# Ten feed-forward blocks by seven products in place of nine, with one of the weight sums added by a DMA

## The chip, the cores and the metric

The kernel runs on one core of a Trainium2 chip. A core has a matrix engine (TensorE, in the profile PE, its weight loads PEld), three engines for elementwise work (VectorE = DVE, ScalarE = ACT, GpSimd = POOL) and a sync engine (SyncE = SP) that here only issues DMAs. The metric is the time of one execution on the device in microseconds; three runs of the kernel before gave a median of 1944.8 us (1944.8 to 1944.86).

## What is computed

Two decoder layers over 256 tokens of width 2048, all in float32. Cut to what matters here:

```python
h  = rms_norm(x, norm1_g[l]);  z = h @ w_in[l]          # then SGU and attention
x  = x + mixed @ w_out[l]
h2 = rms_norm(x, norm2_g[l])
x  = x + (silu(h2 @ w_gate[l]) * (h2 @ w_up[l])) @ w_down[l]
```

`w_gate` and `w_up` are 2048 x 5632, `w_down` is 5632 x 2048. The change is in the last line only.

## The kernel before

**Precision.** A float32 product is made of three matmuls in a rounded float32 form: each operand is split in a high part and a low rest (`ah`, `al`; `wh`, `wl`), and `mm3` (lines 137 to 140) adds high*high, high*low and low*high in PSUM. So every tile of weights has to be split on its way to TensorE: `split2` (lines 93 to 104) has ScalarE make `wh` by a cast (L99) and VectorE make `wl` by a subtraction (L100). There are five buffers each for `wh` and `wl`. Weights arrive as raw tiles of 128 x 1024 (512 KB), seven buffers, loaded by SP (`raw_load`, L90).

**Blocks.** The 5632 columns of the feed-forward part are eleven blocks of 512. For a block, gate and up can be computed in two ways.
- *Standard* (`half`, `even`): 8 raw tiles of `w_gate` and 8 of `w_up`, each a unit of 12 matmuls. 192 matmuls, 16 splits.
- *Seven products* (`seven`, lines 608 to 680): the tokens (two groups of 128), the rows of the weights (even and odd groups of 256) and the two matrices (gate, up) make a 2 x 2 by 2 x 2 product of blocks, done with seven block products in place of eight. The price is sums of weight tiles. B11 and B12 are the even rows of gate and up (`b11`, `b12`), B21 and B22 the odd ones (`b21`, `b22`). There are four steps (`i`), each with five units of 6 matmuls: product 0 of `b11`, product 1 of `b11 + b12`, product 3 of `t2 = b11 + b12 + b22`, product 2 of `b12 + b22`, product 4 of `b22`. VectorE makes the three sums at L636, L637 and L642, in place in the raw tiles but for `t2`. After `t2` has been split for product 3, GpSimd issues a DMA that adds `b21` to it in place (L644, an accumulating DMA). After the four steps eight more units use `b21` (loaded again) and the four `t2`. In all 7 x 24 = 168 matmuls, 28 splits, 12 sums and 7 small operations on VectorE; standard has 2 of these.

Blocks 2 to 10 are made by seven products (`S_BLOCKS`), 0 and 1 the standard way.

**Order.** `s_stream` yields after each unit of the seven-product blocks. Between its units the loop at the end of the layer inserts units of the other stream (`std_stream`, ordered by `STD_ORDER`: gate and up of the standard blocks, and the products with `w_down`, "down", 12 matmuls for one split) as long as a tally of VectorE's work is ahead of TensorE's: `vec` adds 1.14 us for each sum or split, `pe` takes off 0.227 us x `LOAD` for each matmul. The resulting order is fixed when the program is built, and each engine takes its instructions in that order. A raw tile's buffer comes free when its last split is done, and SP, which issues the loads in order, waits for that.

Of the kernel before, what the change touches and what calls it, by code (L numbers as in the profile page):

```python
# [16 lines left out]
ALU = mybir.AluOpType  # L17
# [22 lines left out]
NI = 3584 // NB  # L40
NFF = DFF // NB
ND = D // NB
S_BLOCKS = (2, 3, 4, 5, 6, 7, 8, 9, 10)
STD_ORDER = (
    ("gu", 0), ("down", (0, 2)), ("down", (3, 4)), ("gu", 1), ("down", (1, 5)), ("down", (6, 7)), ("down", (8, 9)), ("down", (10,)),
)
ACTS = 6
HOLD = 2
VEC = 1.14
VEC_P = 0.6  # L50
MM = 0.227
LOAD = 0.95
RL = 512
WARM = 12

# [12 lines left out]
def trunk(ctx, tc, x, xt, w_in, w_out, w_gate, w_up, w_down, sgu_w, sgu_g, consts,  # L68
          rel_bias, onehot, radd, out):
    nc = tc.nc  # L70
# [15 lines left out]
    def raw_load(src, parts=1):  # L86
        raw = wp.tile([P, 2, NB], F32, tag="raw", name="raw", bufs=7)
        n = 2 // parts
        for i in range(parts):
            nc.sync.dma_start(raw[:, i * n : (i + 1) * n, :], src[:, i * n : (i + 1) * n, :])  # L90
        return raw

    def split2(raw):
        wh = wp.tile([P, 2, NB], F32R, tag="wh", name="wh", bufs=5)
        wl = wp.tile([P, 2, NB], F32R, tag="wl", name="wl", bufs=5)
        step = 2 if clock[0] > 1 else 1
        for j in range(0, 2, step):
            src = raw[:, j : j + step, :]
            nc.scalar.copy(wh[:, j : j + step, :], src)  # L99
            nc.vector.tensor_tensor(  # L100
                wl[:, j : j + step, :], src, f(wh[:, j : j + step, :]), ALU.subtract
            )
        vec(1)
        return wh, wl
# [3 lines left out]

    def vec(n, cost=VEC):
        debt[0] += n * cost  # L110

    def pe(n):
        debt[0] -= n * MM * LOAD

# [6 lines left out]
    def tick(w=1.0):  # L121
        clock[0] += w
        due = sorted((e for e in pending if e[0] <= clock[0]), key=lambda e: e[:2])
        pending[:] = [e for e in pending if e[0] > clock[0]]
        for e in due:
            e[2]()
# [10 lines left out]
    def mm3(acc, ah, al, wh, wl, first, last, **more):  # L137
        nc.tensor.matmul(acc, ah, wh, start=first, stop=False, **more)  # L138
        nc.tensor.matmul(acc, ah, wl, start=False, stop=False, **more)  # L139
        nc.tensor.matmul(acc, al, wh, start=False, stop=last, **more)  # L140
# [134 lines left out]
    for lay in range(L):  # L275
# [324 lines left out]
        def act_later(b, sg, held=held, admit=admit):  # L600
            def come(c):
                held.append((b, c, sg))
                admit()

            for c in range(2):
                later(2 + c, lambda c=c: come(c))

        def seven(b, lay=lay, pairs2=pairs2, ext2=ext2, act_later=act_later):
            bank = {}

            def s_unit(raw, m, i, op, first, last, **more):
                wh, wl = split2(raw)
                if m not in bank:
                    bank[m] = pa.tile([P, NB], F32, tag="acc", name=f"m{m}")
                for j in range(2):
                    ah, al = (op(2 * i + j, h) for h in range(2))
                    mm3(bank[m], ah, al, wh[:, j, :], wl[:, j, :], first and j == 0, last and j == 1, **more)
                pe(6)
                tick(0.5)

            def a_op(k, t):
                return lambda p, h: pairs2[p][:, h, k, t * P : (t + 1) * P]

            def e_op(n):
                return lambda p, h: ext2[p][:, h, n, :]

            kept = []
            for i in range(4):
                b11 = raw_load(w_gate[lay, b, i, 0])
                b12 = raw_load(w_up[lay, b, i, 0])  # L630
                b22 = raw_load(w_up[lay, b, i, 1])
                t2 = ap.tile([P, 2, NB], F32, tag="spt", name="t2", bufs=4)
                first, last = i == 0, i == 3
                s_unit(b11, 0, i, a_op(0, 0), first, last)
                yield
                nc.vector.tensor_tensor(b11, b11, b12, ALU.add)  # L636
                nc.vector.tensor_tensor(t2, b11, b22, ALU.add)  # L637
                s_unit(b11, 1, i, e_op(1), first, last)
                vec(1)
                vec(1)  # L640
                yield
                nc.vector.tensor_tensor(b12, b12, b22, ALU.add)  # L642
                s_unit(t2, 3, i, e_op(2), first, last)
                nc.gpsimd.dma_start(t2, w_gate[lay, b, i, 1], accum_op=ALU.add)  # L644
                vec(1)
                yield
                s_unit(b12, 2, i, e_op(0), first, last)
                yield
                s_unit(b22, 4, i, e_op(3), first, last)
                kept.append(t2)  # L650
                yield last
            m1 = zp.tile([P, NB], F32, tag="z", name="m1")
            nc.scalar.copy(m1, bank[0])
            u1 = zp.tile([P, NB], F32, tag="z", name="u1")
            nc.vector.tensor_tensor(u1, bank[3], m1, ALU.add)
            c12 = zp.tile([P, NB], F32, tag="z", name="c12")
            c22 = zp.tile([P, NB], F32, tag="z", name="c22")
            nc.vector.tensor_tensor(c12, bank[1], u1, ALU.add)
            nc.vector.tensor_tensor(c22, bank[2], c12, ALU.add)
            nc.vector.tensor_tensor(c12, bank[4], c12, ALU.add)  # L660
            vec(4, VEC_P)
            yield
            for i in range(5):
                if i < 4:
                    b21 = raw_load(w_gate[lay, b, i, 1])
                    s_unit(b21, 0, i, a_op(1, 0), False, i == 3, skip_group_check=True)
                    yield
                if i > 0:
                    s_unit(kept[i - 1], 2, i - 1, a_op(1, 1), False, i == 4, skip_group_check=True)
                    yield  # L670
            sg = [m1, u1]
            nc.vector.tensor_tensor(u1, bank[2], u1, ALU.add)
            for t, src in ((0, bank[0]), (1, u1)):
                nc.scalar.activation(sg[t], src, AF.Silu, scale=rstd2[t])
            vec(1, VEC_P)
            for t, c in ((0, c12), (1, c22)):
                nc.vector.scalar_tensor_tensor(sg[t], c, nrstd2[t], sg[t], ALU.mult, ALU.mult)
            vec(2, VEC_P)
            act_later(b, sg)
            yield  # L680
# [3 lines left out]
        def s_stream(seven=seven):  # L684
            for b in S_BLOCKS:
                yield from seven(b)
# [77 lines left out]
        for full in s_stream():  # L764
            while (debt[0] > 0.0 or full and len(held) > HOLD) and next(other, False):
                pass
# [92 lines left out]
```

## Time and profile before

| | |
|---|---|
| median of three runs | 1944.8 us |
| profiled execution, time | 1945.16 us |
| profiled execution, span of its instructions | 1943.5 us |
| granted clock of TensorE | 1.0 throughout |
| bytes moved by DMA | 424.43 MB |
| raw loads of `w_gate`, `w_up`, `w_down` | 176 each |
| accumulating DMAs (L644) | 72 |

The profile has one page and views that can be asked of the same trace: the busy time of each engine in given stretches (windows), the groups of instructions by line with what ended the idle time before them, the waits, the DMA queues, and the timeline. Times in rows are microseconds unless ns is said. Matmuls overlap, so a matmul's own duration is longer than the pace at which they follow each other. "<-" in a row's brackets names what ended the wait before it. The rows themselves are shown in the prediction where they are used.

### The profile page before, as it was taken

Reading aid. Unit: us, or ns where it says so; the run is one execution under the profiler, and the core shown is the slowest. Engines: PE = TensorE matmul, PEld = TensorE weight load, DVE = VectorE, ACT = ScalarE, POOL = GpSimd, SP = SyncE. Lnnn points to the kernel's source line nnn. Section 1 sums busy time; section 2 is a strip of 40 time slices with the busy share of each in tenths; the row PEclk is TensorE's granted clock in tenths of the full one; section 3 lists DMA queues with packets and bytes.
Section 4 is the critical chain, followed back from the end, with each engine's and each line's share of the span. In section 5 each row is a group of like instructions: output and inputs, shape, how many; then the busy total and the mean of one; then the engine's idle time right before and its main releaser. Section 6 shows DMA issues by size and latency. Waiting matters only on the chain.

```text
span 1943.5 us, 24615 instructions
## 1 busy us (share of the span) xinstructions
PE 1933.4 (99%) x8894; PEld 1588.5 (82%) x8894; DVE 1699.4 (87%) x1909; ACT 1151.3 (59%) x1455; POOL 127.1 (7%) x137
## 2 busy tenths in 40 slices
PE   9999999999999999999999999999999999999998
PEld 7788888888888888888888888888888888888887
DVE  6787689999999999999767876899999999999995
ACT  7465566666565665665555565666666566665662
POOL 1210001000000000000002100000000000000000
PEclk9999999999999999999999999999999999999999
DMA  8854557768668667767655445577677678768773
GB/s 322 266 174 152 184 170 233 223 226 266 216 215 268 219 229 246 221 226 247 206 194 191 158 163 182 176 247 219 222 243 234 215 244 240 237 217 245 240 239 120
DMA packets 119707, 424.43 MB, mean 218 GB/s; under 512 B 13168, under 2 KB 15344, under 8 KB 119584
## 3 DMA queue, kind: packets, MB, share of 16 engines
q1 hardware_dynamic: 106928, 377.57, 54.6%
q0 software_dynamic: 12512, 45.19, 12.5%
q8 instruction: 70, 1.15, 0.2%
q14 instruction: 53, 0.43, 0.1%
q10 hardware_dynamic: 144, 0.08, 0.0%
HBM read 420.66 MB, written 4.23 MB: 219 GB/s over the span
## 4 chain that ended last, share of the span: by engine, by line
PE 94%; DVE 3%; issue 1%; ACT 1%; DMA 1%; SPq 0%; ACTq 0%; DVEq 0%
PE m L140 11%; PE m L139 11%; PE m L138 11%; PE acc L138 10%; PE acc L140 10%; PE acc L139 10%; PE dacc L138 9%; PE dacc L139 9%; PE dacc L140 9%; DVE wl L100 2%; PE ps_v L399 1%; PE ps_f L208 1%; ACT wh L99 1%; PE ps_s L357 1%; PE ps_t L208 1%
## 5 line engine op out<-in xcount | busy, mean ns | idle before, releaser
L99 ACT CAST wh<-raw 128x1024 fp32r<-128x1024 f32 (+1 forms) x778 | 799.7, 1049 | 607.3 <-DVE raw L636 200.5
L100 DVE TENSOR_TENSOR wl<-raw,wh 128x1024 fp32r<-128x1024 f32 (+1 forms) x778 | 925.4, 1217 | 128.2 <-ACT wh L99 121.1
L138 PE MATMUL m<-wh,ext 128*128 128x512 f32 x576 | 225.7, 392 | 0.0
L138 PE MATMUL dacc<-wh,aT 128*128 128x512 f32 x576 | 225.0, 392 | 0.3
L139 PE MATMUL dacc<-wl,aT 128*128 128x512 f32 x576 | 225.1, 391 | 0.0
L139 PE MATMUL m<-wl,ext 128*128 128x512 f32 x576 | 224.6, 390 | 0.0
L140 PE MATMUL dacc<-wh,aT 128*128 128x512 f32 x576 | 224.5, 390 | 0.0
L140 PE MATMUL m<-wh,ext 128*128 128x512 f32 x576 | 224.3, 389 | 0.0
L100 DVE TENSOR_TENSOR wl<-t,wh 128x1024 fp32r<-128x1024 f32 x144 | 175.2, 1219 | 21.8 <-ACT wh L99 18.1
L99 ACT CAST wh<-t 128x1024 fp32r<-128x1024 f32 x144 | 151.4, 1052 | 57.5 <-PE dacc L140 40.0
L138 PE MATMUL acc<-wh,hT 128*128 128x512 f32 x448 | 180.3, 404 | 0.5 <-ACT wh L99 0.5
L139 PE MATMUL acc<-wl,hT 128*128 128x512 f32 x448 | 175.3, 391 | 0.8 <-DVE wl L100 0.7
L140 PE MATMUL acc<-wh,hT 128*128 128x512 f32 x448 | 175.3, 391 | 0.0
L138 PE MATMUL m<-wh,hT 128*128 128x512 f32 x432 | 168.5, 390 | 0.3 <-ACT wh L99 0.3
L140 PE MATMUL m<-wh,hT 128*128 128x512 f32 x432 | 168.1, 389 | 0.0
L139 PE MATMUL m<-wl,hT 128*128 128x512 f32 x432 | 168.1, 389 | 0.0
L138 PE MATMUL acc<-wh,aT 128*128 128x512 f32 x384 | 151.7, 395 | 0.0
L140 PE MATMUL acc<-wh,aT 128*128 128x512 f32 x384 | 149.9, 390 | 0.0
L139 PE MATMUL acc<-wl,aT 128*128 128x512 f32 x384 | 149.7, 390 | 0.0
L644 POOL DMA_DIRECT2D t<-in_w_gate_dram x72 | 61.5, 854 | 1327.3 <-DVE wl L100 828.5
L138 PEld LDWEIGHTS dacc<-wh,aT 128*128 128x128 f32 x576 | 108.1, 188 | 24.0 <-DVE xres L725 1.6
L139 PEld LDWEIGHTS dacc<-wl,aT 128*128 128x128 f32 x576 | 108.2, 188 | 23.9 <-DVE wl L100 2.2
(142 smaller groups left out, 2832.9 us busy)
## 6 DMA issues: line engine op xcount, KB each, us to landing
raw<-in_w_gate_dram SPq DMA_DIRECT2D x176, 512.0 KB, 5.3
raw<-in_w_up_dram SPq DMA_DIRECT2D x176, 512.0 KB, 4.5
raw<-in_w_down_dram SPq DMA_DIRECT2D x176, 512.0 KB, 4.9
raw<-in_w_in_dram SPq DMA_DIRECT2D x108, 512.0 KB, 4.3
t<-in_w_gate_dram POOLq DMA_DIRECT2D x72, 512.0 KB, 6.3
raw<-in_w_out_dram SPq DMA_DIRECT2D x64, 512.0 KB, 3.2
bias<-rdram POOLq DMA_DIRECT2D x8, 512.0 KB, 5.1
raw<-in_w_in_dram SPq DMA_DIRECT2D x8, 256.0 KB, 5.6
```

The source lines that it names most:

```text
L99: nc.scalar.copy(wh[:, j : j + step, :], src)
L100: nc.vector.tensor_tensor(wl[:, j : j + step, :], src, f(wh[:, j : j + step, :]), ALU.subtract)
L138: nc.tensor.matmul(acc, ah, wh, start=first, stop=False, **more)
L139: nc.tensor.matmul(acc, ah, wl, start=False, stop=False, **more)
L140: nc.tensor.matmul(acc, al, wh, start=False, stop=last, **more)
L208: nc.tensor.transpose(ps[:, j, t * P : (t + 1) * P], blocks[t][:, j * P : (j + 1) * P], ident)
L357: nc.tensor.matmul(halves[r][:, i, :], qT[h // 8][HD * r : HD * r + HD, (h % 8) // 2, t * P : (t + 1) * P], kT[HD * r : HD * r + HD, g, :n ...
L399: nc.tensor.matmul(pv[:, i, :], pt[:, i * nkb + b, :], zkv[b][:, (NKV + g) * HD : (NKV + g + 1) * HD], start=b == 0, stop=b == nkb - 1,)
L644: nc.gpsimd.dma_start(t2, w_gate[lay, b, i, 1], accum_op=ALU.add)
```

## The change

Block 1 is made by seven products too; the standard stream keeps gate and up of block 0 only, and its "down" pieces are regrouped. In all ten blocks the sum `b12 + b22` is no longer made by VectorE but by an accumulating DMA that GpSimd issues after product 1's unit: it reads the tile of B22 a second time from memory and adds it to `b12` in place. Product 2, which needs that sum, moves from fourth to last in each step, behind product 4. The tally no longer counts the sum, and its `LOAD` goes from 0.95 to 0.93.

```diff
-S_BLOCKS = (2, 3, 4, 5, 6, 7, 8, 9, 10)
+S_BLOCKS = (1, 2, 3, 4, 5, 6, 7, 8, 9, 10)
 STD_ORDER = (
-    ("gu", 0), ("down", (0, 2)), ("down", (3, 4)), ("gu", 1), ("down", (1, 5)), ("down", (6, 7)), ("down", (8, 9)), ("down", (10,)),
+    ("gu", 0), ("down", (0, 1)), ("down", (2, 3)), ("down", (4, 5)), ("down", (6, 7)), ("down", (8, 9)), ("down", (10,)),
 )
+T3_DMA = (1, 2, 3, 4, 5, 6, 7, 8, 9, 10)
-LOAD = 0.95
+LOAD = 0.93
...
                 s_unit(b11, 1, i, e_op(1), first, last)
                 vec(1)
                 vec(1)
+                if b in T3_DMA:
+                    nc.gpsimd.dma_start(b12, w_up[lay, b, i, 1], accum_op=ALU.add)
                 yield
-                nc.vector.tensor_tensor(b12, b12, b22, ALU.add)
+                if b not in T3_DMA:
+                    nc.vector.tensor_tensor(b12, b12, b22, ALU.add)
+                    vec(1)
                 s_unit(t2, 3, i, e_op(2), first, last)
                 nc.gpsimd.dma_start(t2, w_gate[lay, b, i, 1], accum_op=ALU.add)
-                vec(1)
+                yield
+                s_unit(b22, 4, i, e_op(3), first, last)
                 yield
                 s_unit(b12, 2, i, e_op(0), first, last)
-                yield
-                s_unit(b22, 4, i, e_op(3), first, last)
                 kept.append(t2)
                 yield last
```

## The prediction

> **What bounds the kernel now.** I read the page's first part, then the busy time by stretches, then the timeline inside a feed-forward stretch.
>
> ```profile
> span 1943.5 us, 24615 instructions
> ...
> PE 1933.4 (99%) x8894; PEld 1588.5 (82%) x8894; DVE 1699.4 (87%) x1909; ACT 1151.3 (59%) x1455; POOL 127.1 (7%) x137
> ```
>
> TensorE is the bound by share. The windows show what that share hides (columns: stretch, its length, busy time of PE, PEld, DVE, ACT, POOL, granted clock, DMA share, GB/s):
>
> ```profile
> 14.00:18.00 4.00, 4.00 (x20) 3.25 (x19) 3.99 (x7) 3.85 (x9) 0.00 (x0) 1.00 1.02 402
> 200.00:250.00 50.00, 50.00 (x231) 41.35 (x230) 32.84 (x44) 28.03 (x42) 1.10 (x2) 1.00 0.53 181
> 290.00:910.00 620.00, 619.32 (x2762) 509.55 (x2762) 598.39 (x584) 381.32 (x407) 32.51 (x38) 1.00 0.74 235
> 1250.00:1895.00 645.00, 644.28 (x2874) 530.61 (x2873) 620.25 (x606) 397.75 (x423) 32.49 (x38) 1.00 0.74 233
> ```
>
> 290 to 910 and 1250 to 1895 are the stretches in which the seven-product blocks are made, one for each layer. There TensorE has no gap, and VectorE is almost as full: it idles 620 - 598.39 = 21.6 us in the one and 645 - 620.25 = 24.75 us in the other, 46.4 us together. ScalarE has 38% to spare. So whatever delays VectorE in these stretches by more than it can spare delays everything.
>
> The pace of a matmul, from the first and the last of 76 that follow each other:
>
> ```profile
> 502.42 0.40 PE L138 MATMUL dacc<-wh,aT 128*128 128x512 f32 x1
> ...
> 519.43 0.39 PE L138 MATMUL m<-wh,ext 128*128 128x512 f32 x1
> ```
>
> 17.01 us / 75 = 0.227 us. The pace of VectorE, from the same stretch:
>
> ```profile
> 497.44 1.28 DVE L725 TENSOR_TENSOR xres<-dacc,xres 128x512 f32<-128x512 f32 x2
> 498.64 5.76 DVE L100 TENSOR_TENSOR wl<-raw,wh 128x1024 fp32r<-128x1024 f32 x5
> 504.43 1.23 DVE L636 TENSOR_TENSOR raw<-raw 128x1024 f32<-128x1024 f32 x1
> 505.69 1.23 DVE L637 TENSOR_TENSOR t<-raw 128x1024 f32<-128x1024 f32 x1
> 506.86 2.36 DVE L100 TENSOR_TENSOR wl<-raw,wh 128x1024 fp32r<-128x1024 f32 x2
> 509.13 1.22 DVE L642 TENSOR_TENSOR raw<-raw 128x1024 f32<-128x1024 f32 x1
> 510.27 1.22 DVE L100 TENSOR_TENSOR wl<-t,wh 128x1024 fp32r<-128x1024 f32 x1
> ```
>
> Five splits in 5.76 us: a split or sum costs 1.15 us of the queue (one overlaps the next a little, so less than its own 1.22), a small operation 0.65.
>
> **TensorE: 10.9 us less.** One block for each layer goes from 192 matmuls to 168: 2 x 24 x 0.227 = 10.9 us. TensorE has no gap in these stretches, so all of it is gained if it stays the bound.
>
> **VectorE: about 30 us less work.** For each layer the change removes 36 sums of L642 (9 blocks x 4), and adds 12 splits (28 in place of 16), 8 sums of L636 and L637 for the tenth block, and 5 small operations: (-36 + 12 + 8) x 1.15 + 5 x 0.65 = -15.1 us. Inside a stretch the count differs a little, because in the instruction order of the changed program 13 fewer units of the other stream lie between the first and the last seven-product unit: splits +28 - 13 = +15, sums +8 - 36, that is -13 x 1.15 + 5 x 0.65 = -11.7 us for VectorE, while TensorE gets 168 - 13 x 12 = 12 matmuls more there, +2.7 us. The room VectorE has before it sets the time is 46.4 + 2 x (11.7 + 2.7) = 75 us.
>
> ScalarE makes 12 more casts for each layer, 2 x 12 x 1.05 = 25 us on an engine with over 230 us idle in each stretch. I take nothing for it. The moved unit is the same 6 matmuls. Its tile `b12` is now given back one unit later and `b22` one earlier; by the order, the shortest cover of a raw load (VectorE's work between the release of its buffer and its first use) goes from 7 operations to 6, about 7 us.
>
> ```profile
> DMA to landing us min/median/max: 3.1/4.9/7.3
> ```
>
> That is the raw loads, 350 to 850 us: they stay just inside, so I take 0 (to +10 us, if some thirty of them come 0.3 us late).
>
> **The DMAs: 88 more, and what they cost if they bind.** Ten blocks x 4 x 2 layers are 80 for `b12`, and 8 for the tenth block's `t2`. In the stretch from 350 to 850 us:
>
> ```profile
> q1 hardware_dynamic: 27884, 101.58, 55.9%
> q0 software_dynamic: 4032, 14.68, 17.0%
> ...
> raw<-in_w_up_dram SPq DMA_DIRECT2D x68, 512.0 KB, 4.4
> raw<-in_w_gate_dram SPq DMA_DIRECT2D x64, 512.0 KB, 5.5
> raw<-in_w_down_dram SPq DMA_DIRECT2D x62, 512.0 KB, 5.1
> t<-in_w_gate_dram POOLq DMA_DIRECT2D x28, 512.0 KB, 6.1
> ```
>
> A plain load takes 0.559 x 500 / 194 = 1.44 us of the sixteen DMA engines, an accumulating one 0.170 x 500 / 28 = 3.04 us. So 44 more for each layer are 134 us more, and the share of 0.74 rises to about (0.74 x 620 + 134) / 623 = 0.95. On average that fits. In the four steps of a block it is tighter: 12 raw loads of its own, 7.8 of the other stream (mean by the new order) and 8 accumulating ones make 19.8 x 1.44 + 8 x 3.04 = 52.8 us, against (120 + 7.8 x 12) x 0.227 = 48.5 us of TensorE. But 1.44 is a price under light load: at 14 to 18 us the queue moved 402 GB/s, 1.30 us for each 512 KB, which makes 50.1 us. The excess of 1.6 to 4.3 us is caught up in the eight units after the steps, which need few loads. I take 0 for throughput; uncovered, 20 x 1.6 to 20 x 4.3 = 32 to 86 us.
>
> **The new wait.** ScalarE's cast of `b12` must now wait for the accumulating DMA to land, and behind it in ScalarE's queue stand the casts of all later tiles, for which VectorE's splits wait, for which TensorE waits. The DMA can be issued when VectorE has done L636 (it reads `b12`). The parts of the way from there to VectorE's split of `b12`:
>
> ```profile
> 511.78 0.86 POOL L644 DMA_DIRECT2D t<-in_w_gate_dram  x1 [12.88 <-DVE wl L100]
> ```
> ```profile
> 507.67 1.05 ACT L99 CAST wh<-t 128x1024 fp32r<-128x1024 f32 x1
> ```
> ```profile
> DMA to landing us min/median/max: 5.0/6.3/8.8
> ```
>
> GpSimd starts 511.78 - (510.27 + 1.22) = 0.29 us after the VectorE instruction it waits for; the DMA of L644 (last row, all 72) lands 6.3 us later; the cast is 1.05; I add 0.06 for the hand-over. That is 7.7 us at today's median, 6.4 and 10.2 at the ends. GpSimd's queue has nothing else in these steps than this DMA and the one of `t2`, so nothing new queues there.
>
> What covers it is VectorE's own work between the sum and the split of `b12`: the sum for `t2`, the splits of product 1, `t2` and `b22`, and what the order puts between. Counted over the 80 steps of the changed program, priced with 1.15 and 0.65: 24 steps have 5.75 or 5.9 us, 16 have 6.4 to 7.05, 14 have 7.55 or 7.7, 8 have 8.2 or 8.35, and 18 have 9.35 or more. VectorE's stall, summed over all steps, is then 15 us for a way of 6.4 us, 62 for 7.7, 101 for 8.4 and 219 for 10.2.
>
> Which landing to take? A plain load shows what a fuller queue does:
>
> ```profile
> raw<-in_w_gate_dram SPq DMA_DIRECT2D x176, 512.0 KB, 5.3
> ...
> raw<-in_w_out_dram SPq DMA_DIRECT2D x64, 512.0 KB, 3.2
> ```
>
> The loads of `w_out` run at a share of about 0.53 (200 to 250 us) and land in 3.2 us, those of `w_gate` at 0.74 in 5.3: 2.1 us for 0.21 of share. Another 0.21 should cost the accumulating DMA something too, but less, since a stalled VectorE also asks for fewer loads. I take 7.0, nearer the median than the maximum: a way of 8.4 us, 101 us of stalls. 75 of them fit in VectorE's room, 25 do not.
>
> Sum, from the profiled execution's 1945.2 us (0.4 above the median of the runs): 1945.2 - 10.9 + 25 = 1959.3, say **1960 us**.
>
> The Trainium skill, page "DMA: Bandwidth & Descriptors", section "Anatomy of one DMA — SWDGE (gpsimd) path", fits a GpSimd-issued DMA as 2.0 us plus the bytes at 436 GB/s, an estimate of 3.2 us for 512 KB. No row here comes near: the fastest of 72 took 5.0. By that fit the way is 4.6 us, no step stalls, and the time would be that of the first rival. The same page, section "SWDGE vs HWDGE vs iDMA", says that each DMA engine takes its queues in turn; this speaks against the change, and is in line with the spread from 5.0 to 8.8 above.
>
> **Rivals.**
> - *The wait is hidden, TensorE stays the bound: faster.* At a landing of 6.3 the stalls are 62 us and the room is 75. For it: VectorE waits for ScalarE only 14 times in 500 us now (columns: total, times, longest), so nothing else uses up the room:
>
> ```profile
> DVE wl L100 <- ACT wh L99: 11.4, 14, 1.5
> ```
>   Against it: the DMA queue gets fuller, as above. Time 1945.2 - 10.9 = 1934. It decides up to a landing of about 6.6 us.
> - *The steps become bound by the DMA queue.* If the excess of the steps isn't caught up, 1945.2 - 10.9 + 86 = 2020. For it: a share of 0.95 with bursts. Against it: 1.02 with 402 GB/s at 14 to 18 us, with VectorE and TensorE full there.
> - *Landings as slow as the slowest now*, 8.8: 219 - 75 = 144, 2078.
> - *Nothing measurable*: stalls of 75 + 11 = 86 us, a landing of about 6.8 us, the gain just paid back.
>
> That the change isn't made as told is excluded by the order: 48 fewer matmuls, 88 more accumulating DMAs, and L642's sum in no step.
>
> **Chances.** Forecast (stalls past the room by 15 to 60 us) 0.46, hidden 0.33, nothing measurable 0.08, queue-bound 0.09, very slow landings 0.04. What can be told from no change is about 0.2%, 4 us. So faster 0.33, same 0.08, slower 0.59. The forecast's own range is 1949 to 1994; with the rivals 1933 to 2015.
>
> **What would show it.** In the profile after: about 1,200 us of seven-product stretches with L642's group gone; waits of ScalarE's cast for the accumulating DMA at the last unit of the steps, above all where no unit of the other stream lies between; its landing near 7.0; a DMA share near 0.92 to 0.95; gaps on PE with releaser wh or wl in the steps. If PE is still without gaps, the forecast is wrong and the first rival right. If ScalarE and VectorE wait for raw loads rather than for the accumulating DMA, it is the queue.

## The result, and the profile after

The changed kernel takes 1991.05 us (median of 4 runs, 1989.23 to 1998.4), the one before beside it 1944.83: a ratio of 1.0245, 95% interval 1.0233 to 1.0257, 2.4% slower. The profiled execution took 1989.23 us.

First part and fourth part (the chain that ended last) of the page after:

```profile
span 1987.5 us, 24959 instructions
...
PE 1943.6 (98%) x8846; PEld 1581.5 (80%) x8846; DVE 1667.3 (84%) x1887; ACT 1171.1 (59%) x1481; POOL 202.5 (10%) x225
...
PE 32%; issue 17%; DVE 8%; DMA 5%; ACT 1%; POOL 1%; POOLq 0%; ACTq 0%; DVEq 0%; SPq 0%
```

The shares of the first row have hardly moved, and by them nothing is wrong: 98% for TensorE. The chain of waits is plainer. Before, 94% of it was TensorE (page before, part 4); now 32% is, and DMAs are 5% of it.

The windows after, for the stretches shown before:

```profile
290.00:910.00 620.00, 599.72 (x2625) 485.32 (x2624) 555.56 (x547) 373.58 (x400) 65.85 (x77) 0.99 0.86 257
1250.00:1895.00 645.00, 629.55 (x2775) 511.92 (x2774) 580.93 (x578) 391.82 (x427) 66.78 (x78) 0.99 0.86 255
```

VectorE's idle time is 64.4 + 64.1 = 128.5 us, where it was 46.4, although it has less to do. TensorE has gaps of 20.3 + 15.5 us, where it had 1.4. The clock column says 0.99 in place of 1.00. The DMA share is 0.86, not the 0.95 that was worked out. In part that is because the stretches have become longer; but in the run with the DMAs beside (below), where TensorE has hardly a gap, the share is 0.90. The prices were taken too high as well: in the first window here a plain load takes 0.513 x 620 / 229 = 1.39 us of the sixteen DMA engines, not 1.44, and an accumulating one 0.347 x 620 / 75 = 2.87 us, not 3.04:

```profile
q1 hardware_dynamic: 32913, 119.83, 51.3%
q0 software_dynamic: 10656, 38.80, 34.7%
```

Who waited for whom, over the whole execution (total, times, longest):

```profile
DVE wl L101 <- ACT wh L100: 212.8, 190, 4.2
...
ACT wh L100 <- DMA raw<-in_w_up_dram: 122.9, 58, 4.8
...
PEld m L140 <- DVE wl L101: 33.5, 42, 1.5
```

The second row is new: 58 casts wait 122.9 us for a DMA of `w_up`, all of them for the accumulating one (the view of L643 names ScalarE's L100 with the same 122.9, 58 as the only one who waited for it). The first row is the next link; before, it was:

```profile
DVE wl L100 <- ACT wh L99: 139.2, 147, 3.6
```

The third is the last link, TensorE. One step in the timeline, VectorE, ScalarE and GpSimd:

```profile
493.71 1.23 DVE L637 TENSOR_TENSOR raw<-raw 128x1024 f32<-128x1024 f32 x1
...
500.68 1.22 DVE L101 TENSOR_TENSOR wl<-raw,wh 128x1024 fp32r<-128x1024 f32 x1
505.15 2.36 DVE L101 TENSOR_TENSOR wl<-raw,wh 128x1024 fp32r<-128x1024 f32 x2 [3.25 <-ACT wh L100]
```
```profile
498.85 1.05 ACT L100 CAST wh<-raw 128x1024 fp32r<-128x1024 f32 x1
504.07 2.01 ACT L100 CAST wh<-raw 128x1024 fp32r<-128x1024 f32 x2 [4.17 <-DMA raw<-in_w_up_dram]
```
```profile
490.56 0.86 POOL L649 DMA_DIRECT2D t<-in_w_gate_dram  x1 [7.20 <-DVE wl L101]
495.23 0.85 POOL L643 DMA_DIRECT2D raw<-in_w_up_dram  x1 [3.81 <-DVE raw L637]
501.06 0.86 POOL L649 DMA_DIRECT2D t<-in_w_gate_dram  x1 [4.98 <-DVE wl L101]
```

The sum of L637 ends at 494.94; GpSimd issues 0.29 us later; the DMA lands 8.74 us after that, at 503.97; the cast starts 0.1 us on, and VectorE, done with everything else at 501.90, starts its split 3.25 us late. So the links and the small terms of the way (0.29, 1.05) are as predicted; for the hand-over the prediction added 0.06 without a row, and here it is 0.10 from the landing to the cast and 0.03 from the cast to the split. The landings of the two accumulating DMAs, L643 first, then L649 (min, median, max):

```profile
DMA to landing us min/median/max: 4.9/5.4/8.7
```
```profile
DMA to landing us min/median/max: 5.3/8.5/9.8
```

The first is *shorter* in the median than the 7.0 us that the prediction took, and than the 6.3 of L644 before. But it is two populations: 46 of the 80 land within 4.9 to 5.6 us, 34 take 5.75 to 8.7 (mean 7.3). When a slow one is issued, at least two raw loads are in flight in all 34 cases, and the previous step's `t2` as well in 32. Of the 46 fast ones 22 find fewer than two raw loads in flight, but 19 find as many and `t2` as well. So a full queue goes with every slow landing, but does not make every landing slow.

VectorE's idle time just before its split of `b12`, added up over the 80 steps of the trace, is 79 us: 44 steps have more than 0.3 us, and 19 with more than 2 us make 57 of the 79.

### The profile page after: what moved, and what is told of

The parts are those of the page before. It is cut to its first block, busy times and chain, and to the rows that moved or that the text cites. A ratio compares the mean times of both kernels' runs of the same rounds, so it can differ in the third digit from the quotient of the medians.

```text
span 1987.5 us, 24959 instructions
## 1 busy us (share of the span) xinstructions
PE 1943.6 (98%) x8846; PEld 1581.5 (80%) x8846; DVE 1667.3 (84%) x1887; ACT 1171.1 (59%) x1481; POOL 202.5 (10%) x225
## 4 chain that ended last, share of the span: by engine, by line
PE 32%; issue 17%; DVE 8%; DMA 5%; ACT 1%; POOL 1%; POOLq 0%; ACTq 0%; DVEq 0%; SPq 0%
PE acc L139 5%; PE acc L141 5%; PE acc L140 5%; DMA raw<-in_w_up_dram 4%; DVE wl L101 4%; PE m L140 3%; PE m L141 3%; PE m L139 2%; PE dacc L139 2%; PE dacc L141 2%; PE dacc L140 2%; DVE raw L637 1%; ACT wh L100 1%; POOL raw L643 1%; DVE t L638 1%
## 5 line engine op out<-in xcount | busy, mean ns | idle before, releaser
L100 ACT CAST wh<-raw 128x1024 fp32r<-128x1024 f32 (+1 forms) x786 | 806.0, 1048 | 638.4 <-DVE raw L637 202.1
L140 PE MATMUL m<-wl,ext 128*128 128x512 f32 x640 | 254.8, 398 | 18.9 <-DVE wl L101 18.6
L139 PE MATMUL m<-wh,ext 128*128 128x512 f32 x640 | 251.7, 394 | 8.2 <-ACT wh L100 8.2
L141 PE MATMUL m<-wh,ext 128*128 128x512 f32 x640 | 250.5, 391 | 0.0
L139 PE MATMUL dacc<-wh,aT 128*128 128x512 f32 x608 | 239.1, 395 | 0.7 <-ACT wh L100 0.7
L141 PE MATMUL dacc<-wh,aT 128*128 128x512 f32 x608 | 238.5, 392 | 0.0
L100 ACT CAST wh<-t 128x1024 fp32r<-128x1024 f32 x160 | 168.2, 1051 | 51.5 <-PE dacc L141 30.5
L101 DVE TENSOR_TENSOR wl<-t,wh 128x1024 fp32r<-128x1024 f32 x160 | 194.1, 1218 | 4.3 <-ACT wh L100 1.6
L139 PE MATMUL m<-wh,hT 128*128 128x512 f32 x480 | 187.0, 390 | 0.0
L140 PE MATMUL m<-wl,hT 128*128 128x512 f32 x480 | 186.8, 389 | 0.0
L141 PE MATMUL m<-wh,hT 128*128 128x512 f32 x480 | 186.8, 389 | 0.0
L140 PEld LDWEIGHTS m<-wl,ext 128*128 128x128 f32 x640 | 120.5, 188 | 57.3 <-DVE wl L101 33.5
L643 POOL DMA_DIRECT2D raw<-in_w_up_dram x80 | 67.9, 848 | 911.7 <-DVE raw L637 842.6
L139 PEld LDWEIGHTS m<-wh,ext 128*128 128x128 f32 x640 | 120.1, 188 | 38.2 <-ACT wh L100 13.8
L141 PEld LDWEIGHTS m<-wh,ext 128*128 128x128 f32 x640 | 120.6, 188 | 23.5
L139 PE MATMUL acc<-wh,aT 128*128 128x512 f32 x352 | 138.8, 394 | 0.0
L141 PE MATMUL acc<-wh,aT 128*128 128x512 f32 x352 | 137.4, 390 | 0.0
```

The costliest lines, as they stand in the source:

```text
L101: nc.vector.tensor_tensor(wl[:, j : j + step, :], src, f(wh[:, j : j + step, :]), ALU.subtract)
L643: nc.gpsimd.dma_start(b12, w_up[lay, b, i, 1], accum_op=ALU.add)
```

## The experiments

Three theories were open. A: the wait of ScalarE's casts for the new DMA. B: the traffic of 88 more DMAs. C: the new order (ten blocks, product 2 last, fewer units of the other stream between). One time each, where nothing else is said; the kernel before took 1944.06 to 1945.39 us beside them.

**Neither sum nor DMA.**

```diff
-    zp = ctx.enter_context(tc.tile_pool(name="zp", bufs=8))
+    zp = ctx.enter_context(tc.tile_pool(name="zp", bufs=6))
...
-                if b in T3_DMA:
-                    nc.gpsimd.dma_start(b12, w_up[lay, b, i, 1], accum_op=ALU.add)
```

> The changed kernel without the accumulating DMA for b12 and without the sum (B22's part of product 2 is left out; two z buffers fewer, as in the next run). Theory A, the wait of the casts for that DMA costs the time: 1934 to 1938 us, the 10.9 us of 48 matmuls gained, PE idle under 3 us in the stretches. Rival B, the traffic of the extra DMAs: 1934 to 1938 too. Rival C, the new order itself (ten blocks, product 2 last, fewer units of the other stream inside): 1975 to 1990.

Measured: 1935.84 us. TensorE idles 2.7 + 1.8 = 4.5 us in the two windows, VectorE 36.4 + 38.6 = 75.0 us:

```profile
290.00:910.00 620.00, 617.31 (x2756) 508.04 (x2755) 583.59 (x572) 394.42 (x420) 36.06 (x42) 1.00 0.76 238
1250.00:1895.00 645.00, 643.16 (x2873) 529.32 (x2872) 606.37 (x597) 411.62 (x439) 36.05 (x42) 1.00 0.77 239
```

Without sum and DMA, the ten blocks in the new order are good for 1944.65 - 1935.84 = 8.8 us, most of the predicted 10.9. C, the order by itself, is out. This run and the next have six `z` buffers in place of eight; no run shows what that alone is worth.

**The DMAs beside the kernel's work.**

```diff
-    zp = ctx.enter_context(tc.tile_pool(name="zp", bufs=8))
+    zp = ctx.enter_context(tc.tile_pool(name="zp", bufs=6))
...
+    spare = cp.tile([P, 2, NB], F32, tag="spare", name="spare")
+    nc.vector.memset(spare, 0.0)
...
                 nc.vector.tensor_tensor(b11, b11, b12, ALU.add)
+                nc.vector.tensor_copy(spare[:, 0, 0:1], b11[:, 0, 0:1])
...
-                    nc.gpsimd.dma_start(b12, w_up[lay, b, i, 1], accum_op=ALU.add)
+                    nc.gpsimd.dma_start(spare, w_up[lay, b, i, 1], accum_op=ALU.add)
```

> As the run without sum, but the 80 accumulating DMAs are issued as in the changed kernel, at the same time (after a copy of one column, which follows the sum b11 + b12), into a spare tile that nobody reads, so no cast waits for them (B22's part of product 2 is left out). Theory A: 1936 to 1945. Rival B, traffic: 1980 to 1995, with ScalarE and VectorE waiting for raw loads.

Measured: 1937.73 us. The same traffic at the same time costs 1.9 us when nobody waits for it. The windows show a fuller queue than in the changed kernel:

```profile
290.00:910.00 620.00, 618.27 (x2759) 508.57 (x2758) 585.90 (x612) 394.89 (x420) 69.37 (x81) 1.00 0.90 271
```

A share of 0.90, 271 GB/s, and TensorE idles 1.7 us in this window. The spare tile's DMA lands later here, 7.3 us in the median, which costs nothing. B is out. What is left for the wait is 1991 - 1937.7 = 53 us.

**The sum on VectorE in all ten blocks, tally counting it.**

```diff
-T3_DMA = (1, 2, 3, 4, 5, 6, 7, 8, 9, 10)
+T3_DMA = ()
```

> The changed kernel with the sum made by VectorE in all ten blocks (the set of blocks with the DMA empty, the tally counts the sum). Theory A: VectorE gets 80 x 1.15 = 92 us of work back, of which about 25 us fit: 1945 to 1975, gaps spread over the steps, no waits for an accumulating DMA. Rival C, the order: 1985 or more.

Measured: 2102.39 us, far outside what either theory expected. The instruction order tells why: the tally now asks for more units of the other stream, uses up what is there by the fourth block, and later blocks get 0 or 16 in turns, since the next "down" units need blocks that aren't made yet. So this run says nothing of the sum itself; it shows that the tally's balance is worth more than all that is studied here.

**Nine blocks with the DMA** (and the streams of before).

```diff
-S_BLOCKS = (1, 2, 3, 4, 5, 6, 7, 8, 9, 10)
+S_BLOCKS = (2, 3, 4, 5, 6, 7, 8, 9, 10)
...
-LOAD = 0.93
+LOAD = 0.95
```

> The DMA sum and product 2 last, but nine blocks with the streams and LOAD of before. Theory A: 72 of the 80 waits stay, 48 matmuls come back: 1980 to 1995. Rival C, the tenth block is at fault: 1945 to 1950.

Measured: 2089.22 us, a miss of the same kind: without the sum in its tally and with LOAD 0.95 the order as built has 0 to 6 units of the other stream between the first and the last unit of a block's four steps (before: 7 to 9), and 39 behind the last block of a layer (before: 17). The next run has, beside these changes, the tally of before:

```diff
-                    vec(1)
+                vec(1)
                 s_unit(t2, 3, i, e_op(2), first, last)
```

> Nine blocks, streams, LOAD and tally of before (the tally still counts the sum, so the units of the other stream stand where they stood), only the sum by DMA and product 2 last. The earlier nine-block run took 2089 us with a tally without the sum, which put five to eight units into the steps of a block where before has seven to ten. Theory A: the wait alone, somewhat better covered: 1960 to 1985. If 2089 came from the DMA itself: 2050 or more.

Measured: 1953.77 us, a little better than expected. Here the four steps of a block have 7 to 9 units of the other stream between them, as before, where the changed kernel has 5 to 7. The 72 DMAs cost about 9 us in all against the kernel before, and casts wait 70.3 us in place of 122.9.

```profile
ACT wh L100 <- DMA raw<-in_w_up_dram: 70.3, 37, 4.4
```

**`t2`'s DMA behind the next step's DMA for `b12`.**

```diff
+                for late, n in held_t2:
+                    nc.gpsimd.dma_start(late, w_gate[lay, b, n, 1], accum_op=ALU.add)
+                held_t2 = [(t2, i)]
...
-                nc.gpsimd.dma_start(t2, w_gate[lay, b, i, 1], accum_op=ALU.add)
+                if last:
+                    nc.gpsimd.dma_start(t2, w_gate[lay, b, i, 1], accum_op=ALU.add)
```

> The changed kernel, but t2's accumulating DMA is issued behind the next step's DMA for b12, so that it is never in flight when that one starts. Theory A with the landing slowed by t2's DMA: b12's DMA lands in 5.0 to 5.6 us in nearly all steps in place of 6 to 8.7 in 34 of 80, the stalls fall from 79 us to about 25: 1945 to 1962. If the raw loads slow the landing, not t2's DMA: 1980 to 1992.

Measured: 1999.69 us, above what either theory expected, and the landing of `b12`'s DMA is

```profile
DMA to landing us min/median/max: 5.3/5.5/9.7
```

But the change did not do what it was meant to do. In the trace GpSimd still issues `t2`'s DMA (now L646) ahead of the next step's DMA for `b12` (L644), 4.7 us ahead here, as in the changed kernel (490.56 and 495.23 above):

```profile
489.25 0.86 POOL L646 DMA_DIRECT2D t<-in_w_gate_dram  x1 [7.20 <-DVE wl L101]
493.92 0.85 POOL L644 DMA_DIRECT2D raw<-in_w_up_dram  x1 [3.81 <-DVE raw L638]
```

Over the whole trace the two kinds alternate just as in the changed kernel. So this run is little more than the changed kernel once more, and whether `t2`'s transfer or the raw loads make the slow landings slow stays open.

**A plain copy in place of the adding one.**

```diff
-                    nc.gpsimd.dma_start(b12, w_up[lay, b, i, 1], accum_op=ALU.add)
+                    nc.gpsimd.dma_start(b12, w_up[lay, b, i, 1])
```

> The changed kernel, but the DMA on GpSimd's queue copies B22 over b12 in place of adding it (so product 2 gets B22 alone). It keeps the wait, the queue and the issue, and halves the DMA engines' time. Theory A: landing 4 to 5 us, a way of about 6 us, stalls of 10 to 25 us, time 1938 to 1955. If the issue through GpSimd or t2's DMA in flight makes the landing slow rather than the adding: 1970 to 1990.

Measured: 1944.97 us. Landing, and the casts' wait:

```profile
DMA to landing us min/median/max: 3.6/5.1/7.1
```
```profile
ACT wh L100 <- DMA raw<-in_w_up_dram: 61.3, 44, 2.9
```

The median is only 0.3 us shorter, the maximum 1.6; the casts' waits are halved and none is over 2.9 us, and all but 7 of the 53 us are gone. So the slow landings cost, not the typical one. VectorE's stalls before its split of `b12` come to some 34 us here, three of them over 2 us; sum and longest fell together, so this run doesn't tell which of the two counts.

**Product 2 one step later.**

```diff
+                if due is not None:
+                    s_unit(due, 2, i - 1, e_op(0), i == 1, False)
+                    yield
+                due = b12
...
-                yield
-                s_unit(b12, 2, i, e_op(0), first, last)
+                if last:
+                    yield
+                    s_unit(b12, 2, i, e_op(0), first, last)
```

> The changed kernel, but product 2 of a step is made in the next step behind product 1 (the last one at the end of the block), so four more VectorE operations, 4.6 us, cover the DMA, and b12's raw buffer is held as much longer. Theory A: the casts hardly wait, 1936 to 1945. Rival, the seven raw buffers become the limit: casts and sums wait for raw loads, 1955 to 1990.

Measured: 1949.99 us. Its two waits for DMAs:

```profile
ACT wh L100 <- DMA raw<-in_w_down_dram: 36.7, 21, 3.8
ACT wh L100 <- DMA raw<-in_w_up_dram: 35.6, 17, 3.5
```

The time lies between what the theory and its rival expected. The wait for `b12` has shrunk to less than a third, but `b12` now holds its raw buffer longer, and casts wait as much for loads of `w_down`, which in the changed kernel they did not. Both the theory and its rival have a part. So the same with one raw buffer more:

```diff
-    zp = ctx.enter_context(tc.tile_pool(name="zp", bufs=8))
+    zp = ctx.enter_context(tc.tile_pool(name="zp", bufs=6))
...
-        raw = wp.tile([P, 2, NB], F32, tag="raw", name="raw", bufs=7)
+        raw = wp.tile([P, 2, NB], F32, tag="raw", name="raw", bufs=8)
```

> Product 2 one step later as before (1950 us with seven raw buffers), now with eight raw buffers and six z buffers. If the rest of the loss against 1937.7 us came from late raw loads: 1936 to 1943, faster than the kernel before. If it came from the casts that still wait for b12's DMA (36 us in all): 1946 to 1952.

Measured: 1938.15 us (1936.11 to 1938.44, 5 runs) against 1944.75 before; ratio 0.9962, interval 0.9948 to 0.9976. This version is faster than both kernels, by 0.4% than the one before, and within 2.3 us of the one without the sum. It still has waits for `b12`'s DMA, all thirteen in the last step of a block, where product 2 has no next step to go to:

```profile
ACT wh L100 <- DMA raw<-in_w_up_dram: 30.0, 13, 2.9
```

**The sum on VectorE, every unit at its place.**

```diff
-                if b in T3_DMA:
-                    nc.gpsimd.dma_start(b12, w_up[lay, b, i, 1], accum_op=ALU.add)
                 yield
-                if b not in T3_DMA:
-                    nc.vector.tensor_tensor(b12, b12, b22, ALU.add)
-                    vec(1)
+                nc.vector.tensor_tensor(b12, b12, b22, ALU.add)
```

> Ten blocks, product 2 last and the tally of the changed kernel (the sum isn't counted), but VectorE makes the sum: no DMA, no wait, 80 x 1.15 = 92 us more of VectorE's work at the same place in the order. If VectorE had 75 us of room, as the prediction had it: 1934 + 17 = 1951. If its idle time outside the steps is no room and only the work removed is (about 25 us), as theory A has it after the first runs: about 1934 + 67 = 2001.

Measured: 1964.94 us, between the two. 92 us more of VectorE's *work*, 1.15 us in each step, cost 1964.9 - 1935.8 = 29 us, so 63 us of it found room. That is close to the 75 us of the prediction. 79 us of *waiting* cost 53. At this place the DMA is dearer than the sum that it replaces.

**The DMA directly behind the raw load** (with eight raw and six `z` buffers, as two runs above; the main lines).

```diff
+            def sum_load(i):
+                b12 = raw_load(w_up[lay, b, i, 0])
+                nc.gpsimd.dma_start(b12, w_up[lay, b, i, 1], accum_op=ALU.add)
+                return b12
...
+                nc.vector.tensor_tensor(t2, b11, b12, ALU.add)
+                nc.vector.tensor_tensor(b11, t2, b22, ALU.subtract)
```

> B22 is added to b12 by the DMA directly behind b12's raw load, a step ahead; VectorE makes t2 = b11 + b12 and then b11 = t2 - b22, so no sum stands before the DMA, product 3 comes before product 1; eight raw and six z buffers. Theory A: the way from the load to the first use is long enough, 1936 to 1945. Rival: the raw load and the accumulating DMA in a row (5 + 6 to 9 us) are longer than the cover, and now VectorE's first sum of the step waits: 1955 to 2000.

Measured: 2066.79 us (2064.51 to 2067.66, 4 runs). The rival holds in kind, and costs more than it expected:

```profile
POOL raw L630 <- DMA raw<-in_w_up_dram: 402.2, 38, 58.7
...
DVE t L642 <- DMA raw<-in_w_up_dram: 81.6, 27, 7.2
```

Now VectorE itself stands before the DMA, up to 7.2 us at a time, with all its splits behind.

**The DMA in every other block, no sum in the rest.**

```diff
-                if b in T3_DMA:
+                if b % 2:
```

> The changed kernel with the DMA for b12 in blocks 1, 3, 5, 7 and 9 only; in the others the sum is left out (product 2 gets b12 alone), so every unit stands where it stood and half of the waits are gone. If VectorE's room can be used wherever it is free, as the prediction had it, 40 us of stalls fit in it: 1935 to 1941. If a stall costs at its place as soon as the five wh and wl buffers run dry, half of the 53 us stays: 1958 to 1968.

Measured: 1960.81 us (1959.06 to 1962.68, 4 runs). Half of the waits leave 1960.8 - 1937.7 = 23 of the 53 us. Its windows:

```profile
290.00:910.00 620.00, 608.91 (x2691) 495.85 (x2690) 570.39 (x560) 383.12 (x411) 51.37 (x60) 1.00 0.84 249
1250.00:1895.00 645.00, 635.26 (x2821) 519.03 (x2820) 596.50 (x592) 400.53 (x431) 53.13 (x62) 1.00 0.83 247
```

VectorE idles 49.6 + 48.5 = 98 us in them, and TensorE has gaps of 11.1 + 9.7 = 20.8 us all the same. Room in a block without waits does not serve a block with them.

## Why the prediction was right in kind and wrong in size

- **TensorE, -10.9 us: right.** The order without sum and DMA gains 8.8 us.
- **VectorE's work, about 30 us less: right.** Its busy time fell from 1699.4 to 1667.3 us.
- **No cost for the traffic: right.** 1.9 us, by the DMAs beside. The sums from 1.44 and 3.04 us for each DMA, which came to more than the steps have, did not bind. The queue-bound rival is out.
- **The wait and what is queued behind it: right,** link by link in the timeline: L637, GpSimd, landing, cast, split, TensorE.
- **The landing, taken as 7.0: off, and in part made good by luck.** The median is 5.4, a way of 6.8 us, for which the prediction's own figures give between 15 and 62 us of stalls. The stalls came to 79, because 34 of the 80 landings average 7.3 where one landing was taken for all. So 79 lies near the predicted 101 since two errors work against each other.
- **"75 of them fit in VectorE's room, 25 do not": this is the step that failed.** Of 79 us of stalls only 79 - 53 = 26 us were absorbed, and the term measured 53 us where 25 were forecast: 28 of the 32 us between the forecast 1959 and the measured 1991. The room itself was sized right: without sum and DMA, VectorE idles 75.0 us in the two windows. But it was a sum of idle time over two stretches of over 600 us, and stalls were set against it as if they could be moved there. Spread work can, for the most part: 63 of 92 us fitted when VectorE made the sums itself. The every-other-block run shows that waits do not share it.

  Nor does the length of a stall alone decide. What VectorE has to do next goes with it. Of the 19 stalls of over 2 us in the trace after, 13 stand two splits ahead of the next step's two sums, which give TensorE nothing to do; TensorE has gaps of 0.5 to 3.2 us around 12 of these (from 2 us before the late split to 8 us behind its start). The other six stand in the last step of a block, with twelve or more splits ahead of the next sum. Around five of these TensorE has no gap, although the two longest stalls of all are among them. One of each, VectorE and then the window behind it:

```profile
318.83 2.36 DVE L101 TENSOR_TENSOR wl<-raw,wh 128x1024 fp32r<-128x1024 f32 x2 [3.02 <-ACT wh L100]
321.22 1.23 DVE L637 TENSOR_TENSOR raw<-raw 128x1024 f32<-128x1024 f32 x1
322.48 1.22 DVE L638 TENSOR_TENSOR t<-raw 128x1024 f32<-128x1024 f32 x1
...
735.33 1.23 DVE L101 TENSOR_TENSOR wl<-raw,wh 128x1024 fp32r<-128x1024 f32 x1 [4.19 <-ACT wh L100]
736.75 2.36 DVE L101 TENSOR_TENSOR wl<-raw,wh 128x1024 fp32r<-128x1024 f32 x2 [0.20 <-ACT wh L100]
```
```profile
318.80:326.80 8.00, 5.75 (x21) 3.88 (x20) 7.90 (x7) 5.18 (x6) 0.84 (x1) 0.92 0.99 259
735.30:743.30 8.00, 8.00 (x36) 6.07 (x35) 7.77 (x9) 7.33 (x8) 0.00 (x0) 1.00 1.04 357
```

  Behind the stall of 3.02 us TensorE is busy 5.75 of 8 us, behind that of 4.19 all the time. The version with product 2 one step later and eight raw buffers agrees: nine stalls of over 2 us are left in it, up to 3.2, all in the last step of a block, with no gap of TensorE around any. In that version and in the every-other-block run VectorE's stalls before the split of `b12` come to some 35 us each. The first, with its long ones at the ends of blocks, is 2.3 us behind the run without the sum; the second, with most of its long ones ahead of sums, is 23 us behind the one with the DMAs beside. 778 to 782 us in the trace after shows VectorE catching up after a stall, the two sums among its work: it is busy all the time, TensorE a third of it.

```profile
778.30:781.60 3.30, 1.15 (x4) 0.37 (x2) 3.30 (x4) 2.63 (x3) 0.84 (x1) 1.00 1.00 309
```

  This is read from the traces; no run changed only what follows a stall. How much the five `wh` and five `wl` buffers cover was not tried either.
- **TensorE's clock** was in no term. In the profiled execution it was halved five times for 3.41 us, 17 us at half pace, an estimate of 8.5 us of matmuls lost. That is a part of the 53.
- **The outer range, 1933 to 2015,** leaves out the times of two of the prediction's own rivals, 2020 and 2078.

The Trainium skill's fit in "DMA: Bandwidth & Descriptors" (section "Anatomy of one DMA — SWDGE (gpsimd) path"), an estimate of 3.2 us for 512 KB, is not met here even by the plain copy, 3.6 us at the least and 5.1 in the median.

In one line: 1944.65 - 8.8 (ten blocks, no sum) + 1.9 (traffic) = 1937.7 us, + 53 (waits, most of the long ones ahead of sums) = 1991.

## What to carry to other kernels

Idle time of an engine is room for more work, spread evenly; it isn't room for waits. When work is handed to a DMA, compare the slowest landings, not the median, with the cover of the step that has least of it, and look at what the waiting engine has to do next: a wait is dear where the work behind it gives the bound engine nothing. If the cover is too short, move the use a step later, and give the tile that is held longer a buffer of its own: that turned 2.4% slower into 0.4% faster. And look in the trace whether a change meant for the order has changed it.

## What the runs showed of the hardware that was not expected

TensorE's granted clock falls to half for 3.41 us at a time, though no gap of TensorE in the feed-forward stretches was longer than 2.15 us. The five times (at 325.5, 550.8, 782.9, 1649.9 and 1765.9 us) begin whole multiples of 3.413 us apart. If the trace is cut into windows of this length that end where the first begins, each of the five follows a window in which TensorE idles 1.5 to 2.1 us. The window that idles most without being followed by one has 1.46. Two that are followed by one (the first with the half-clock window behind it), then the one with 1.46:

```profile
322.09:325.50 3.41, 1.90 (x8) 1.03 (x7) 3.38 (x4) 2.94 (x4) 0.84 (x1) 1.00 0.99 291
325.50:328.91 3.41, 3.41 (x10) 2.67 (x9) 3.41 (x4) 3.00 (x5) 0.35 (x1) 0.50 0.99 294
547.37:550.78 3.41, 1.29 (x6) 0.73 (x4) 3.41 (x6) 0.90 (x2) 0.00 (x0) 1.00 0.84 271
714.62:718.03 3.41, 1.95 (x8) 1.07 (x7) 3.41 (x4) 3.41 (x4) 0.84 (x1) 1.00 0.79 186
```

So here it goes by the idle time in such a window, with the dividing line near 1.5 us; in some of the other runs single windows with 1.5 to 1.9 us of idle time were not followed by one. The Trainium skill, "TensorE: Matmul & The Clock Gate", section "HAM oscillation — how this bites in real kernels", gives as its rule no idle gaps of more than about 3.4 us; by the trace, shorter gaps do it too. In the run with the DMA directly behind the load the mean granted clock was 0.983.

`t2`'s DMA landed in 6.3 us in the median before and in 8.5 in the changed kernel. That is not the doing of `b12`'s DMA: in the run with neither sum nor DMA it is

```profile
DMA to landing us min/median/max: 5.1/8.5/9.8
```

What in the new order makes it slower stays open.
